# Regrouping the expert rows of a two-layer encoder: sorted lists of 80 and 40 rows, 8 rows whole, gate passes of 80 and 48 rows

## The chip, the cores and the metric

The kernel runs on one core of one Trainium2 chip. The metric is the device time of one execution in microseconds; the profile gives the span from the first to the last instruction, and at each point what the engines did. The engines are named as in the profile: PE is TensorE (with PEld, its weight loads), DVE VectorE, ACT ScalarE, POOL GpSimd and SP SyncE.

## The reference

Two layers, each a token mixer (two attention branches, gates, an output projection) and then PEER, a retrieval feed-forward over 128 x 128 = 16384 experts. The change lies in PEER alone. For 256 tokens, in two chunks of 128:

```python
q = (xc @ w_query).reshape(PEER_CHUNK, PEER_HEADS, 2, half)
s = jnp.einsum('thpk,pnk->thpn', q, sub_keys).astype(jnp.float32)
sv, si = lax.top_k(s, PEER_TOPK)
...
top_s, sel = lax.top_k(cand, PEER_TOPK)
eidx = jnp.take_along_axis(cidx, sel, axis=-1)
g = jax.nn.softmax(top_s, axis=-1)
u = expert_down[eidx]
vv = expert_up[eidx]
act = jax.nn.gelu(jnp.einsum('td,thkd->thk', xc, u).astype(jnp.float32), approximate=False)
return jnp.einsum('thk,thkd->td', (g * act).astype(x.dtype), vv)
```

Each token picks 8 heads x 16 experts. Expert e = 128 i + j; i is called its row here.

## The kernel before, in words

The kernel does not gather per token. In the **downs** (L1313 to L1315) it multiplies all 256 tokens with every row of `expert_down`: 64 blocks of two rows, so 128 units, each of 24 matmuls of 256 columns. GELU (L1253, L1257) is put on the result, in the tile `act` (128 experts of a row on the partitions, rows and tokens along them). The **gates** (g of each expert and token, zero where it was not picked) are made by one-hot matmuls, in two passes over the tokens of 64 rows each. A group of 8 tokens builds a one-hot of j (`ej`, DVE L1026, its scaled copy `el` on ACT L1029), one of i (`ei`, L1031) and two products with g (`ag`, L1035). It then runs 24 matmuls: L1048 (which experts are used, `cnt`), L1051 and L1054 (gates). The result is multiplied into `act` (L1067, L1071, or L1263 where the gate was there before the GELU).

Then the **ups** (L1347) multiply `act` with `expert_up`. A block is 128 experts; each chunk of 128 tokens that uses a block costs one block pass of six matmuls of 512 columns. So that few blocks are needed, rows are sorted. For each list of rows a **rank** is worked out from `cnt` (`rank_lane`: PE L1112, L1117 and L1121, a copy on ACT L1114, DVE L1124 to L1133): used experts get places in the order "first chunk only, both, second chunk only". Then POOL **sends** each row of `act` with one indirect DMA to its places in DRAM (L1161). SP **reads back** sorted blocks (L1191), and POOL **fetches** the 128 rows of `expert_up` that belong to a block with one indirect DMA (L1220). `LISTS` holds for each list: first row, rows, blocks in all, blocks that the first chunk uses, and the block from which the second chunk starts. The rows of `WHOLE` are not sorted: a row is a block as it stands, used by both chunks, and fetched by SP with a plain DMA (L1217).

Each weight or expert block is loaded into `raw` (4 buffers, and 6 more inside `act` during the ups) and **split** into two parts, `wh` (ACT L189) and `wl` (DVE L192); a block of `act` is split the same way (ACT L1236, DVE L1238). Splits run up to four units ahead of PE.

Every engine works through its instructions in the order in which they were written. That order comes from a planner (`Lanes`), which keeps an estimated clock for PE, DVE and ACT and places each step where these clocks say it is ready; `main(emit, 0.655, u)` is the planner's cost of six matmuls. A send is tied to a split by `pace`, so that sends are spread over time. If a list has more used experts than its blocks hold, a slow path (`make_up`) does the rest.

In the ups of each layer list 0 comes first, a block for both chunks and a block for one in turn; then the whole rows, then list 1 in the same turns, and at the end list 1's blocks for the second chunk alone (8 of them, before and now).

Of the kernel before, what the change touches and what calls it, by code (L numbers as in the profile page):

```python
# [10 lines left out]
F32 = mybir.dt.float32  # L11
F32R = mybir.dt.float32r
F16 = mybir.dt.float16
# [42 lines left out]
def vcost(n):  # L56
    return 0.1 + n * 0.00105


def scost(n):  # L60
    return 0.12 + n * 0.00084


class Lanes:
# [8 lines left out]
    def __init__(self):  # L73
        self.clk = {"p": 0.0, "v": 0.0, "s": 0.0}
        self.lanes = []
        self.urgent = 0
# [60 lines left out]
    def idle(self):  # L137
        assert self.lanes
        self.clk["p"] += 0.2
        self.pump()  # L140
# [74 lines left out]
def encoder_kernel(ctx, tc, x_in, wts, downs, ups, gains, gate_bias, qk_norm, rpb, sink, skeys, consts, sums, out,  # L215
# [71 lines left out]
    def main(fn, cost, unit=None):  # L287

        fn()
        lanes.use("p", cost, st.ready[unit] if unit is not None else 0.0)  # L290
        lanes.pump()
# [12 lines left out]
    scr = cpool.tile([128, 704], F32, name="scr")  # L304
# [157 lines left out]
    for l in range(depth):  # L462
# [395 lines left out]
        ejs = [pp.tile([128, 4, 128, 2], F16, name=f"ej{i}") for i in range(2)]  # L858
        els = [pp.tile([128, 4, 128, 2], F16, name=f"el{i}") for i in range(2)]
        eis = [pp.tile([128, 4, 64, 2], F16, name=f"ei{i}") for i in range(2)]  # L860
        ags = [pp.tile([128, 2, 4, 64, 2], F16, name=f"ag{i}") for i in range(2)]
# [94 lines left out]
        def index_lane():  # L956
# [50 lines left out]
            number_experts(64, 128)  # L1007
# [5 lines left out]

        NG = T // 8
        cnts, counted, gates, gelus = {}, [0, 0], [0, 0], [0]

        def gate_group(r, n, o):


            i0, w = LISTS[r][:2]  # L1020
            p0 = 64 * r
            ej, el, ei, ag = ejs[o], els[o], eis[o], ags[o]
            tj = ijT[:, 1, 8 * n:8 * n + 8].rearrange("p (a s) -> p a s", s=2)
            ti = ijT[:, 0, 8 * n:8 * n + 8].rearrange("p (a s) -> p a s", s=2)
            yield ("v", 0.68)
            nc.vector.tensor_tensor(ej, iota2[:, None, :, :].to_broadcast([128, 4, 128, 2]),  # L1026
                                    tj[:, :, None, :].to_broadcast([128, 4, 128, 2]), op=OP.is_equal)
            t1 = yield ("s", 1.04)
            nc.scalar.activation(el, ej, AF.Copy, scale=LOW)  # L1029
            yield ("v", 1.25, t1 - 1.0)  # L1030
            nc.vector.tensor_tensor(ei, iota2[:, None, p0:p0 + 64, :].to_broadcast([128, 4, 64, 2]),  # L1031
                                    ti[:, :, None, :].to_broadcast([128, 4, 64, 2]), op=OP.is_equal)
            for k in range(2):
                tg = gT[:, k, 8 * n:8 * n + 8].rearrange("p (a s) -> p a s", s=2)
                nc.vector.tensor_mul(ag[:, k], ei, tg[:, :, None, :].to_broadcast([128, 4, 64, 2]))  # L1035
# [9 lines left out]
            yield ("p", 0.75)  # L1045
            half, t0 = n // 16, 8 * (n % 16)
            for t in range(8):
                nc.tensor.matmul(cnts[r][:, half * w:(half + 1) * w], ej[:, t // 2, :, t % 2],  # L1048
                                 ei[:, t // 2, i0 - p0:i0 - p0 + w, t % 2], start=counted[r] == 0 and t == 0,
                                 stop=counted[r] == NG - 1 and t == 7, skip_group_check=True)  # L1050
                nc.tensor.matmul(b[:, t * 64:(t + 1) * 64], ej[:, t // 2, :, t % 2],  # L1051
                                 ag[:, 0, t // 2, :, t % 2], start=t == 0, stop=False, skip_group_check=True)
            for t in range(8):
                nc.tensor.matmul(b[:, t * 64:(t + 1) * 64], el[:, t // 2, :, t % 2],  # L1054
                                 ag[:, 1, t // 2, :, t % 2], start=False, stop=t == 7, skip_group_check=True)
# [7 lines left out]
            bv = b.rearrange("p (t i) -> p i t", i=64)  # L1063
            g = min(max(2 * gelus[0] - p0, 0), 64)
            if g < 64:
                t = lanes.use("s", scost(8 * (64 - g)), lanes.cur - 0.5)
                nc.scalar.activation(act[:, p0 + g:p0 + 64, half, t0:t0 + 8], bv[:, g:64], AF.Copy)  # L1067
            if g:
                t = lanes.use("v", vcost(8 * g) - 0.35, t if g < 64 else 0.0)
                a = act[:, p0:p0 + g, half, t0:t0 + 8]  # L1070
                nc.vector.tensor_mul(a, a, bv[:, 0:g])  # L1071
            give(b, "s")
            gates[r] += 1
            if gates[r] == NG:
                for k in range(32 * r, min(gelus[0], 32 * r + 32)):
                    done["row", k] = t

        def gate_lane():
            yield from lane_need(["idx"])
            for r in range(2):  # L1080
                for n in range(NG):
                    o = yield from buf_take("oh")
                    lanes.add(gate_group(r, n, o), after=lanes.cur)

        def rank_lane(r, cnt):
# [5 lines left out]
            def f16(off, n):  # L1091
                return scr.bitcast(F16)[:, 2 * off:2 * off + n]
# [4 lines left out]
            m = f16(256, 4 * w).rearrange("p (k i) -> p k i", k=4)  # L1097
            cs = f16(384, 512).rearrange("p (k j) -> p k j", k=4)
            place = f32(384, 4 * w).rearrange("p (k i) -> p k i", k=4)
            rk = f32(640, w)  # L1100
# [43 lines left out]
        def send_lane(r):  # L1144
# [3 lines left out]

            while r and st.nd < up0 + len([x for x in seq if x[1] == 0]):
                yield None  # L1150
            pace = len(st.splits) - 3.0
            for i in range(i0, i0 + w):
# [17 lines left out]
                pace += (0.4, 0.6)[r]  # L1170
# [73 lines left out]
        def gelu_lane(b, acc):  # L1244
# [4 lines left out]
            r, av = b // 32, acc.rearrange("p (a t) -> p a t", a=2)  # L1249

            g = 8 * gates[r]
# [15 lines left out]
            if gates[r] == NG:  # L1267
                done["row", b] = t
# [32 lines left out]
        for b in range(64):  # L1301
# [4 lines left out]
            for ii in range(2):  # L1306
                h, lo = st.get(u)
                o = acc[:, ii * 256:(ii + 1) * 256]
                for k in range(4):
# [6 lines left out]
                    main(emit, 0.655, u)  # L1316
# [202 lines left out]
```

## Time and profile before

| | |
|---|---|
| median of 3 runs | 1838.83 us (1836.73 to 1839.68) |
| the profiled execution | 1839.15 us, span 1837.3 us |
| clock granted to PE, mean | 0.997 |
| layer 1: downs and ups on PE | 244 to 658, 658 to 925 us of the span |
| layer 2: downs and ups on PE | 1158 to 1572, 1572 to 1834 us |
| block passes in the ups, each layer | 79 (list 0) + 56 (whole) + 45 (list 1) = 180 |

The passes follow from `LISTS`: list 0 has 53 blocks, of which blocks 13 to 38 are used by both chunks (26 x 2) and 27 by one. In a timeline of the profile a row gives start, duration, engine, line, operation, output and input; in brackets stands how long the engine had been idle and what ended that. A PE row's duration overlaps with the next, so the cost of a stream is read from start to start.

### The profile page before, as it was taken

Reading aid. Unit: us, or ns where it says so; the run is one execution under the profiler, and the core shown is the slowest. Engines: PE = TensorE matmul, PEld = TensorE weight load, DVE = VectorE, ACT = ScalarE, POOL = GpSimd, SP = SyncE. Lnnn points to the kernel's source line nnn. Section 1 sums busy time; section 2 is a strip of 40 time slices with the busy share of each in tenths; the row PEclk is TensorE's granted clock in tenths of the full one; section 3 lists DMA queues with packets and bytes.
Section 4 is the critical chain, followed back from the end, with each engine's and each line's share of the span. In section 5 each row is a group of like instructions: output and inputs, shape, how many; then the busy total and the mean of one; then the engine's idle time right before and its main releaser. Section 6 shows DMA issues by size and latency. Waiting matters only on the chain. (4 is left out here: it accounts for less than half of the span.)

```text
span 1837.3 us, 38009 instructions
## 1 busy us (share of the span) xinstructions
PE 1808.9 (98%) x14826; PEld 1646.7 (90%) x14826; DVE 1475.7 (80%) x3054; ACT 1081.3 (59%) x1726; POOL 437.0 (24%) x374
## 2 busy tenths in 40 slices
PE   8999999999999999999999999999999999999998
PEld 7889899999999988888778988999999999888886
DVE  6986899988887897756689778998888888976565
ACT  5665554566566666645546654546666666666554
POOL 0000000000038556744200000000000485567341
PEclk9999999999999999999999999999999999999999
DMA  7535456655567889987464354556554688889873
GB/s 259 166 105 175 149 164 193 187 163 158 155 184 247 242 275 295 323 282 225 161 221 144 108 162 159 165 190 199 159 156 156 189 249 245 277 295 327 260 229 122
DMA packets 125139, 372.98 MB, mean 203 GB/s; under 512 B 16528, under 2 KB 38672, under 8 KB 124944
## 3 DMA queue, kind: packets, MB, share of 16 engines
q1 hardware_dynamic: 91440, 256.93, 45.5%
q0 software_dynamic: 33504, 113.47, 17.9%
q8 instruction: 120, 1.97, 0.4%
q14 instruction: 75, 0.61, 0.1%
HBM read 342.87 MB, written 27.47 MB: 202 GB/s over the span
## 5 line engine op out<-in xcount | busy, mean ns | idle before, releaser
L192 DVE TENSOR_TENSOR wl<-raw,wh 128x1024 fp32r<-128x1024 f32 x478 | 581.0, 1222 | 154.7 <-ACT wh L189 152.8
L189 ACT ACTIVATE wh<-raw 128x1024 fp32r<-128x1024 f32 x478 | 505.8, 1059 | 270.1 <-PE bank L1347 79.0
L1313 PE MATMUL bank<-TT,wh 128*128 128x256 f32 x2048 | 582.9, 285 | 0.0
L1314 PE MATMUL bank<-TT,wh 128*128 128x256 f32 x2048 | 572.2, 279 | 0.0
L1315 PE MATMUL bank<-TT,wl 128*128 128x256 f32 x2048 | 571.5, 279 | 0.0
L1347 PE MATMUL bank<-wh,TT 128*128 128x512 f32 x1416 | 394.7, 398 | 8.6 <-PEq L1362 5.8
L1313 PEld LDWEIGHTS bank<-TT,wh 128*128 128x128 f32 x2048 | 384.8, 188 | 0.3
L1314 PEld LDWEIGHTS bank<-TT,wh 128*128 128x128 f32 x2048 | 384.4, 188 | 0.0
L1315 PEld LDWEIGHTS bank<-TT,wl 128*128 128x128 f32 x2048 | 384.2, 188 | 0.0
L1347 PEld LDWEIGHTS bank<-wh,TT 128*128 128x128 f32 x1416 | 265.0, 188 | 75.3 <-issue 7.2
L1161 POOL DMA_INDIRECT rows<-act,rank x200 | 234.2, 1171 | 371.6 <-DVE miss L1133 311.3
L192 DVE TENSOR_TENSOR wl<-act,wh 128x1024 fp32r<-128x1024 f32 x132 | 161.5, 1225 | 97.2 <-ACT wh L189 90.8
L1347 PE MATMUL bank<-wl,TT 128*128 128x512 f32 x708 | 224.3, 396 | 0.4 <-issue 0.4
L189 ACT ACTIVATE wh<-act 128x1024 fp32r<-128x1024 f32 x132 | 139.7, 1060 | 115.6 <-PE bank L1347 106.8
L871 POOL IOTA act<- 128x128 uint32 x4 | 1.7, 437 | 766.5 <-DVE gT L1005 352.5
L1347 PEld LDWEIGHTS bank<-wl,TT 128*128 128x128 f32 x708 | 133.6, 189 | 32.2
L1029 ACT ACTIVATE el<-ej 128x1024 f16<-128x1024 f16 x128 | 133.8, 1053 | 31.1 <-DVE ej L1026 30.3
L1220 POOL DMA_INDIRECT act<-in_ups_dram,act x96 | 118.0, 1229 | 98.5 <-DVE TT L1238 85.1
L1257 ACT ACTIVATE act<-bank 128x256 f32<-128x256 f32 (+8 forms) x238 | 74.5, 362 | 108.3 <-PE bank L1315 106.4
L435 PE MATMUL bank<-TT,wh 128*128 128x256 f32 x448 | 128.6, 287 | 1.7 <-ACT raw_ka L564 1.0
L437 PE MATMUL bank<-TT,wh 128*128 128x256 f32 x448 | 125.1, 279 | 0.0
L438 PE MATMUL bank<-TT,wl 128*128 128x256 f32 x448 | 125.0, 279 | 0.0
(252 smaller groups left out, 2725.7 us busy)
## 6 DMA issues: line engine op xcount, KB each, us to landing
raw<-in_downs_dram SPq DMA_DIRECT2D x256, 512.0 KB, 4.1
raw<-in_wts_dram SPq DMA_DIRECT2D x132, 512.0 KB, 4.2
act<-in_ups_dram SPq DMA_DIRECT2D x36, 512.0 KB, 5.5
act<-rows SPq DMA_DIRECT2D x82, 129.0 KB, 4.5
raw<-in_ups_dram SPq DMA_DIRECT2D x20, 512.0 KB, 5.5
act<-rows SPq DMA_DIRECT2D x84, 64.5 KB, 5.0
rows<-act,rank POOLq DMA_INDIRECT x200, 5.4
Sq<-in_rpb_dram SPq DMA_DIRECT2D x2, 876.0 KB, 7.1
```

The source lines that it names most:

```text
L189: self.nc.scalar.activation(h, r, AF.Copy)
L192: self.splits.append(self.nc.vector.tensor_sub(lo, r, h.bitcast(F32)).ins.name)
L435: nc.tensor.matmul(o, wh, rh, start=first and i == 0 and pc == 0, stop=False, skip_group_check=True)
L437: nc.tensor.matmul(o, wh, rl, start=False, stop=False, skip_group_check=True)
L438: nc.tensor.matmul(o, wl, rh, start=False, stop=last and i == len(kcs) - 1 and pc == 1, skip_group_check=True)
L1029: nc.scalar.activation(el, ej, AF.Copy, scale=LOW)
L1161: snd = nc.gpsimd.indirect_dma_start(byrank[r], bass.IndirectOffsetOnAxis(ap=rank[:, i:i + 1], axis=0), afl[:, i * ROW:(i + 1) * ROW], None)
L1220: nc.gpsimd.indirect_dma_start(w, None, ups_rows, bass.IndirectOffsetOnAxis(ap=num, axis=0), element_offset=l * 16384 * D)
L1313: nc.tensor.matmul(o, lh, TT[:, :, 0, kc, :], start=kc == 0, stop=False)
L1314: nc.tensor.matmul(o, lh, TT[:, :, 1, kc, :], start=False, stop=False)
L1315: nc.tensor.matmul(o, ll, TT[:, :, 0, kc, :], start=False, stop=kc == 7)
L1347: nc.tensor.matmul(oacc[ch][hf], a, r[:, hf * 512:(hf + 1) * 512], start=first[hf] and a is lh and r is h, stop=last and a is ll)
```

## The change

List 0 grows from 64 rows to 80 (66 blocks, 33 of them for both chunks), list 1 from 36 rows to 40 (33 blocks, 17 for both), and 8 rows instead of 28 stay whole. List 0 has 66 + 33 = 99 block passes, the whole rows 16, list 1 33 + 17 = 50: 165 in each layer. A layer sends 120 rows instead of 100, and splits 107 blocks instead of 111.

The gate passes are cut to fit: pass 0 covers rows 0 to 79 in groups of six tokens (20 of six and 2 of four in each chunk, 44 in all), pass 1 rows 80 to 127 in 32 groups of eight. During pass 0 four sets of one-hot buffers stand ready instead of two; two of them lie in rows of `act` that pass 0 does not use yet (from row 114, `LATE`), and POOL numbers these rows' experts after pass 0.

The sends of list 1 no longer wait until all fetches of list 0 are out. They begin when the first ten blocks are on their way, one for each 1.8 splits. Last, the planner's cost of six matmuls in the downs is 0.7 instead of 0.655.

```diff
-LISTS = [(0, 64, 53, 39, 13), (92, 36, 30, 22, 7)]
-WHOLE = (64, 28)
+LISTS = [(0, 80, 66, 49, 16), (88, 40, 33, 25, 8)]
+WHOLE = (80, 8)
+
+PASSES = [(0, 80, [6] * 20 + [4] * 2), (80, 48, [8] * 16)]
...
+LATE = 114
...
+        oh = [pp.tile([128, 1744], F32, name=f"oh{i}") for i in range(2)] + \
+             [afl[:, i * ROW:i * ROW + 1744] for i in (LATE, LATE + 7)]
...
+            p0, pw, _ = PASSES[r]
...
         def gate_lane():
             yield from lane_need(["idx"])
             for r in range(2):
-                for n in range(NG):
+                if r:
+
+                    while len(free["oh"]) < 4:
+                        yield None
+                    number_experts(LATE, 128)
+                    free["oh"] = deque(x for x in free["oh"] if x[0] < 2)
+                    done["late"] = lanes.clk["p"]
+                else:
+                    free["oh"] = deque((i, 0.0) for i in range(4))
+                for n in range(len(toks[r])):
...
-            while r and st.nd < up0 + len([x for x in seq if x[1] == 0]):
+            whole = up0 + len([x for x in seq if x[1] == 0])
+            while r and st.nd < up0 + DEEP:
                 yield None
...
-                while int(pace) >= len(st.splits) and tries < 15:
+                while int(pace) >= len(st.splits) and tries < 15 and lanes.stuck < 5:
...
-                pace += (0.4, 0.6)[r]
+
+                pace += 0.4 if r == 0 else 1.8 if st.nd < whole else 0.6
...
-                    main(emit, 0.655, u)
+                    main(emit, 0.7, u)
```

How POOL's queue reads in the ups of the first layer. Before, from list 0's sends (L1161, `rows` is the sorted copy in DRAM) through its last fetches (L1220):

```order
L1161 DMA rows_2250<-act,rank 8192x258 x64
L1220 DMA raw<-in_ups_dram,act 128x1024 x4
L1220 DMA act<-in_ups_dram,act 128x1024 x6
```

```order
L1220 DMA raw<-in_ups_dram,act 128x1024 x3
L1161 DMA rows_2251<-act,rank 4608x258 x36
L1220 DMA raw<-in_ups_dram,act 128x1024 x3
L1220 DMA act<-in_ups_dram,act 128x1024 x6
L1220 DMA raw<-in_ups_dram,act 128x1024 x4
```

The same place now (sends are L1183, fetches L1243):

```order
L1183 DMA rows_2244<-act,rank 10240x258 x80
L1243 DMA raw<-in_ups_dram,act 128x1024 x4
L1243 DMA act<-in_ups_dram,act 128x1024 x6
L1243 DMA raw<-in_ups_dram,act 128x1024 x2
L1183 DMA rows_2245<-act,rank 5120x258
L1243 DMA raw<-in_ups_dram,act 128x1024
L1183 DMA rows_2245<-act,rank 5120x258 x2
L1243 DMA raw<-in_ups_dram,act 128x1024
L1243 DMA act<-in_ups_dram,act 128x1024 x2
L1183 DMA rows_2245<-act,rank 5120x258
```

There are now 80 sends ahead of the first fetch instead of 64, and list 1's sends stand between the fetches of list 0 (32 of them there, the last 8 behind its last fetch) instead of in one row of 36 behind them.

How ACT's queue reads where the ups begin in the first layer. `wh<-act` at L1236 is the split of the first sorted block, the `wh<-raw` behind it that of the first block of `expert_up`. Before:

```order
L1029 ACTIVATE el_2244<-ej_2242 128x1024
L1253 ACTIVATE bank_8912<-bank_8912 128x2x200
L1257 ACTIVATE act<-bank_8912 128x2x56
L1236 ACTIVATE wh<-act 128x256
L1236 ACTIVATE wh<-act 128x128
L189 ACTIVATE wh<-raw 128x1024
L1029 ACTIVATE el_2245<-ej_2243 128x1024
```

Now (the split of the sorted block is L1259, that of the unit L194, and L1136 is the copy of list 1's counts in `rank_lane`, L1114 before):

```order
L1043 ACTIVATE oh_2242<-oh_2242 128x1024
L1080 ACTIVATE act<-bank_9304 128x4x8
L1278 ACTIVATE bank_9240<-bank_9240 128x512
L1259 ACTIVATE wh<-act 128x256
L1259 ACTIVATE wh<-act 128x128
L194 ACTIVATE wh<-raw 128x1024
L1136 ACTIVATE scr<-bank_7060 40x512
L194 ACTIVATE wh<-raw 128x1024
```

All gate groups now stand ahead of the first up block, and the copy of list 1's counts stands directly behind that block's split; before, it stood 13 splits later, within the ups. On PE, the matmuls of list 1's rank that wait for this copy stand half a unit ahead of the end of the downs, where before they stood 16 passes into the ups. Counted in PE's order in the same way, the last matmul of list 0's rank stands behind 90 units of the downs before and behind 91.25 now, and the second transposes of the picked indices (L995 before, L1005 now) behind 44.5 units and now 40.75.

More of the change, by code (lines that the diff above doesn't have):

```diff
@@ L75, in __init__ @@
         self.lanes = []
+        self.stuck = 0
         self.urgent = 0
@@ L139, in idle @@
         self.clk["p"] += 0.2
+        self.stuck += 1
         self.pump()
@@ L303, in encoder_kernel @@
     nst = cpool.tile([128, 2, 8], F32, name="nst")
-    scr = cpool.tile([128, 704], F32, name="scr")
+    scr = cpool.tile([128, 832], F32, name="scr")
     def bcast_row(src, off, n):
@@ L857, in encoder_kernel @@
         gT = pp.tile([128, 2, T], F16, name="gT")
[L858 to L861, printed above, removed]
+        oh = [pp.tile([128, 1744], F32, name=f"oh{i}") for i in range(2)] + \
+             [afl[:, i * ROW:i * ROW + 1744] for i in (LATE, LATE + 7)]
+        oh = [x.bitcast(F16) for x in oh]
+        ejs, els = [[x[:, k * 1024:(k + 1) * 1024].rearrange("p (a j s) -> p a j s", a=4, s=2) for x in oh] for k in (0, 1)]
+        eis = [x[:, 2048:2528] for x in oh]
+        ags = [x[:, 2528:3488].rearrange("p (k n) -> p k n", k=2) for x in oh]
         A0 = 64 * ROW
@@ L1010, in index_lane @@
             preload(AF.Gelu)
-        NG = T // 8
+        toks = [[(h, sum(g[:k]), n) for h in range(2) for k, n in enumerate(g)] for _, _, g in PASSES]
         cnts, counted, gates, gelus = {}, [0, 0], [0, 0], [0]
@@ L1044, in gate_group @@
             b, = yield from lane_take("s")
-            yield ("p", 0.75)
-            half, t0 = n // 16, 8 * (n % 16)
-            for t in range(8):
+            yield ("p", 0.095 * nt)
+            for t in range(nt):
                 nc.tensor.matmul(cnts[r][:, half * w:(half + 1) * w], ej[:, t // 2, :, t % 2],
                                  ei[:, t // 2, i0 - p0:i0 - p0 + w, t % 2], start=counted[r] == 0 and t == 0,
-                                 stop=counted[r] == NG - 1 and t == 7, skip_group_check=True)
-                nc.tensor.matmul(b[:, t * 64:(t + 1) * 64], ej[:, t // 2, :, t % 2],
+                                 stop=counted[r] == NG - 1 and t == nt - 1, skip_group_check=True)
+                nc.tensor.matmul(b[:, t * pw:(t + 1) * pw], ej[:, t // 2, :, t % 2],
                                  ag[:, 0, t // 2, :, t % 2], start=t == 0, stop=False, skip_group_check=True)
-            for t in range(8):
-                nc.tensor.matmul(b[:, t * 64:(t + 1) * 64], el[:, t // 2, :, t % 2],
-                                 ag[:, 1, t // 2, :, t % 2], start=False, stop=t == 7, skip_group_check=True)
+            for t in range(nt):
+                nc.tensor.matmul(b[:, t * pw:(t + 1) * pw], el[:, t // 2, :, t % 2],
+                                 ag[:, 1, t // 2, :, t % 2], start=False, stop=t == nt - 1, skip_group_check=True)
             counted[r] += 1
@@ L1062, in gate_group @@
             t = yield ("v", 0.35)
[L1063 to L1067, printed above, removed]
+            bv = b[:, 0:nt * pw].rearrange("p (t i) -> p i t", i=pw)
+            g = min(max(2 * gelus[0] - p0, 0), pw)
+            if g < pw:
+                t = lanes.use("s", scost(nt * (pw - g)), lanes.cur - 0.5)
+                nc.scalar.activation(act[:, p0 + g:p0 + pw, half, t0:t0 + nt], bv[:, g:pw], AF.Copy)
             if g:
-                t = lanes.use("v", vcost(8 * g) - 0.35, t if g < 64 else 0.0)
-                a = act[:, p0:p0 + g, half, t0:t0 + 8]
+                t = lanes.use("v", vcost(nt * g) - 0.35, t if g < pw else 0.0)
+                a = act[:, p0:p0 + g, half, t0:t0 + nt]
                 nc.vector.tensor_mul(a, a, bv[:, 0:g])
@@ L1074, in gate_group @@
             if gates[r] == NG:
-                for k in range(32 * r, min(gelus[0], 32 * r + 32)):
+                for k in range(p0 // 2, min(gelus[0], (p0 + pw) // 2)):
                     done["row", k] = t
@@ L1096, in rank_lane @@
             use = f16(192, 2 * w).rearrange("p (c i) -> p c i", c=2)
[L1097 to L1100, printed above, removed]
+            m = f16(192 + w, 4 * w).rearrange("p (k i) -> p k i", k=4)
+            cs = f16(192 + 3 * w, 512).rearrange("p (k j) -> p k j", k=4)
+            place = f32(192 + 3 * w, 4 * w).rearrange("p (k i) -> p k i", k=4)
+            rk = f32(192 + 7 * w, w)
             if r == 0:
@@ L1248, in gelu_lane @@
             t = yield ("s", scost(512))
-            r, av = b // 32, acc.rearrange("p (a t) -> p a t", a=2)
-            g = 8 * gates[r]
+            if 2 * b >= LATE:
+                yield from lane_need(["late"])
+            r, av = int(2 * b >= PASSES[1][0]), acc.rearrange("p (a t) -> p a t", a=2)
+            g = sum(n for _, _, n in toks[r][:gates[r]])
             if g:
@@ L1266, in gelu_lane @@
             gelus[0] += 1
-            if gates[r] == NG:
+            if g == T:
                 done["row", b] = t
```

33 lines of the change are left out of this document (19 added, 14 removed).

## The prediction

> **What bounds the kernel now.** I read the page's first part first, then the stretches of one layer, then the waits of PE.
>
> ```profile
> PE 1808.9 (98%) x14826; PEld 1646.7 (90%) x14826; DVE 1475.7 (80%) x3054; ACT 1081.3 (59%) x1726; POOL 437.0 (24%) x374
> ```
>
> ```profile
> core 0: us, PE busy (x) PEld busy (x) DVE busy (x) ACT busy (x) POOL busy (x), PEclk, DMA share, GB/s
> 244.00:374.00 130.00, 130.00 (x1107) 130.00 (x1106) 123.84 (x361) 69.79 (x104) 0.00 (x0) 1.00 0.60 187
> 374.00:530.00 156.00, 155.89 (x1888) 154.16 (x1887) 134.96 (x236) 98.29 (x150) 0.44 (x1) 1.00 0.51 157
> 530.00:658.00 128.00, 127.49 (x1555) 126.09 (x1552) 107.35 (x196) 83.32 (x139) 89.72 (x75) 1.00 0.79 241
> 658.00:925.00 267.00, 260.36 (x1213) 207.32 (x1209) 182.36 (x271) 152.98 (x236) 127.76 (x109) 0.99 0.79 256
> ```
>
> ```profile
> PE bank L1347 <- PEq L1362: 5.8, 2, 3.4
> PE bank L355 <- DVE z L393: 3.8, 2, 2.9
> ```
>
> PE is the bound everywhere: it idles 28 of 1837 us, and the longest of its waits adds up to 5.8 us. In the downs (244 to 658) nothing waits at all. DVE is second, at 95% of the first stretch (the top-k), 87% of the second (pass 0 of the gates) and 84% of the third (pass 1). So work taken from PE is gained, as long as no other queue becomes late. The one queue that the change loads in a new way is POOL's, so I read that next, with PE's stream beside it.
>
> ```profile
> 527.65 0.46 PE L1121 MATMUL bank<-scr 64*128 64x64 f16 x10
> 528.05 0.38 PE L1313 MATMUL bank<-TT,wh 128*128 128x256 f32 x1
> ...
> 655.32 0.28 PE L1313 MATMUL bank<-TT,wh 128*128 128x256 f32 x1
> ...
> 655.67 0.28 PE L1313 MATMUL bank<-TT,wh 128*128 128x256 f32 x1
> ...
> 656.49 0.41 PE L1054 MATMUL bank<-ag,el 128*128 128x64 f16 x8
> ...
> 658.25 0.70 PE L1347 MATMUL bank<-wh 128*128 128x512 f32 x2
> 658.79 0.63 PE L1347 MATMUL bank<-wl,wh 128*128 128x512 f32 x2
> 659.26 0.62 PE L1347 MATMUL bank<-wh 128*128 128x512 f32 x2
> ```
>
> List 0's rank ends on PE at 528.05, and the ups begin at 658.25. Three matmuls of the downs take 0.353 us from start to start (655.32 to 655.67), so a unit of 24 takes 2.82. Two of the ups' take 0.47 (658.79 to 659.26), so a block pass of six takes 1.40.
>
> ```profile
> 530.46 2.04 POOL L1161 DMA_INDIRECT rows<-act,rank  x1 [155.66 <-DVE miss L1133]
> ...
> 602.80 1.43 POOL L1161 DMA_INDIRECT rows<-act,rank  x1 [0.30 <-issue]
> ...
> 626.44 0.96 POOL L1161 DMA_INDIRECT rows<-act,rank  x1 [0.30 <-DVE wl L192]
> 637.51 0.97 POOL L1220 DMA_INDIRECT raw<-in_ups_dram,act  x1 [10.11 <-DVE act L1263]
> ...
> 707.07 1.71 POOL L1220 DMA_INDIRECT raw<-in_ups_dram,act  x1 [1.25 <-DVE TT L1238]
> 709.08 0.94 POOL L1220 DMA_INDIRECT raw<-in_ups_dram,act  x1 [0.30 <-issue]
> 711.27 1.71 POOL L1220 DMA_INDIRECT act<-in_ups_dram,act  x1 [1.25 <-DVE TT L1238]
> ...
> 751.08 1.00 POOL L1161 DMA_INDIRECT rows<-act,rank  x1 [0.30 <-issue]
> ...
> 800.10 0.96 POOL L1161 DMA_INDIRECT rows<-act,rank  x1 [0.31 <-issue]
> ```
>
> Behind the rank comes a chain that PE does not see yet. 64 sends run from 530.46 to 626.44, back to back with 0.30 between them: 95.98 us in 63 steps, 1.524 each, and 1.576 over the last 15 steps (602.80 to 626.44). In the ups 36 sends take 35 steps from 751.08 to 800.10, 1.40 each. The first fetch goes out at 637.51, and PE needs its block at 658.25: some 13 us of slack, once landing and split are taken off.
>
> **The change part by part**, for one layer; both layers are alike.
>
> *Block passes.* 180 become 165. 15 x 1.40 = **21.0 us less** on PE, all on the path, since PE is the bound of that stretch. The four splits that go with it lie on DVE and ACT beside PE, worth nothing.
>
> *Gate matmuls.* Pass 0 has the same 768 matmuls (three a token), 80 columns wide for 64. Eight of 64 columns start 0.031 us apart ((0.41 - 0.19) / 7, the last one's own length taken off). By columns, 80 would take 0.039. Nothing at all is the other end, since 0.031 is long for 64 columns beside the downs' 0.118 for 256. I take 5 ns each, +3.8 us, and +1.2 for twelve more groups at 0.1. Pass 1 narrows from 64 to 48, between 0 and -3; I take -1. Together **+4** (0 to +7).
>
> *DVE in top-k and pass 0.* The picked indices are transposed 3.75 units earlier in PE's order, which is 10.6 us; DVE has four splits less before that, 4 x 1.15 = 4.6 us.
>
> ```profile
> 368.75 0.29 DVE L991 TENSOR_TENSOR act<-act 128x128 f32<-128x128 f32 x1
> 368.96 1.22 DVE L192 TENSOR_TENSOR wl<-raw,wh 128x1024 fp32r<-128x1024 f32 x1
> ...
> 371.83 0.49 PE L995 MATMUL bank<-cst,act 128*128 128x128 f32 x3
> ```
>
> DVE was ready at 369.0 and PE came at 371.83; 2.8 - 10.6 + 4.6 makes PE wait 3.2 us. Some of DVE's idle 6 us there may be used up instead, so I take **+2** (0 to +5). In pass 0 DVE gets five more splits (6 us), a quarter more of `ei` and `ag` (10), and 18 more products in the GELU (7): 158 of about 169 us, 93%. That is tight, and still covered by splits that run ahead.
>
> *The handover to the ups.* This is the term that decides. All 80 sends must land before the first read-back. Counted from the end of list 0's rank on PE: first send +2.4 (530.46 - 528.05), 79 steps of 1.524 to the last one, at 122.8.
>
> ```profile
> 633.34 6.64 SPq L1191 DMA_DIRECT2D act<-rows  x12
> DMA to landing us min/median/max: 3.0/5.4/7.2
> DMA to landing us min/median/max: 4.2/5.8/8.5
> 683.70 0.59 ACT L1114 ACTIVATE scr<-bank 36x512 f16<-36x512 f32 x1 [0.47 <-PE bank L1112]
> 686.75 0.30 DVE L1124 TENSOR_TENSOR scr<-bank,scr 128x144 f32<-128x144 f32 x1
> ...
> 688.08 0.27 DVE L1133 TENSOR_REDUCE miss<-scr 128x1 f16<-128x108 f32 x1
> ```
>
> (The landings are those of the sends and of the fetches.) The last send lands 3.0 to 6.9 us later (before, the read-back came 6.9 later, behind a load of the downs in SP's queue); I take 4.0, since the downs' loads are over by then: 126.8. Read-back to fetch +4.2 (633.34 to 637.51): 131.0. The fetch lands 4.2 to 5.8 later, taken as 4.5: 135.5. Then ACT splits the block (1.06), and only then copies list 1's counts (0.59), for which PE waits half a unit ahead of the end of the downs: 137.2. PE's matmuls of that rank (0.6) and DVE's chain for it (686.75 to 688.35, 1.6), which PE waits for once more, and hops bring it to **140**. Without waiting PE would be there at 130: before it took 130.2 (528.05 to 658.25) for 38 units and 28 groups. Now 1.25 units go (-3.5), four groups come (0.83 each, +3.3; -1 as they are narrower), and list 1's rank comes (+1). So PE stands **+10** where it stood for nothing. Ends: at 1.40 a step the stall is gone (-9.8); at 1.576 a step, 6.9 and 5.8 it is 10 + 4.1 + 2.9 + 1.3 = 18. The price of a step is that of the same place in the program, so I keep the middle.
>
> The Trainium skill, in the page "SBUF — State Buffer", section "SBUF: two separate sides", says that GpSimd cannot write the descriptors of its DMAs while DVE holds the port the two share, and waits until DVE is done. The trace agrees: an indirect DMA takes 0.94 to 0.96 us with DVE idle and 1.71 where it starts together with a `wl` split. By that rule a step is 1.26 with DVE idle and no stall follows; with DVE as busy as now, 1.52 stays.
>
> *Sends between fetches.* In list 0's stage a pair of blocks takes PE 4.20 us (707.07 to 711.27), and POOL two fetches, 3.25 with gaps. Now 1.11 sends a pair come in (one per 1.8 splits). At 1.40 each of 3.11 steps is 4.35, at 1.26 it is 3.92, and with a full 1.40 on top of 3.25 it is 4.8. Over the 27 pairs behind the first fetches this is 0 to 16 us too slow; some 8 us of it are covered, as ten blocks are fetched ahead. I take **+1** (0 to +8).
>
> ```profile
> 682.00:751.00 69.00, 69.00 (x308) 54.99 (x307) 50.76 (x78) 42.99 (x66) 42.68 (x33) 1.00 0.88 288
> 751.00:806.00 55.00, 55.00 (x237) 44.32 (x236) 34.84 (x46) 31.17 (x47) 39.32 (x36) 1.00 0.96 327
> ```
>
> DMA carried 288 GB/s there. 32 sends of 132 KB in 139 us add 30: 318, under the 327 that the second row shows without PE waiting.
>
> *The rest.* The iota behind pass 0 (0.4 us on POOL), wider `scr` and two more buffer sets lie beside other work, and the last blocks of a layer stay as they are. Nothing.
>
> Sum: -21 + 4 + 2 + 10 + 1 = -4 a layer, -8 in all. The profiled execution took 1839.15 us (1.85 more than its span), 0.3 above the median of 1838.83, so the forecast is **1831 us**. A measurement of this kernel tells 0.2%, 3.7 us, from no change.
>
> **The rivals.**
>
> *A: the handover costs nothing.* If DVE leaves POOL more room at the end of the downs and a step is 1.40, the stall goes: -21 + 4 + 2 = -15 a layer, 1809 us. For it: the sends of the ups ran at 1.40 with DVE less busy. Against: the rate is the same in both layers, and steps got longer towards the end (1.576), when `act` is multiplied most.
>
> *B: slower, by the handover alone.* The first block's arrival behind 80 sends decides from a stall of 16 us a layer on, that is a mean step over 1.60 with the rest as taken, or 1.576 with the late landings. With a stall of 18 the sum is +4 a layer: 1847 us. For it: the last 15 steps at 1.576, and the added sends are at that end. Against: the downs' loads are over by then.
>
> *C: POOL cannot carry fetches and sends together.* At 4.8 us a pair PE waits in list 0's stage, +8 a layer instead of +1: 1845 us. For it: a fetch that starts with DVE's split took 1.71. Against: a late POOL finds its buffers free, and DVE slows with PE.
>
> *D: the change does not shorten PE's work,* because a list overflows and the slow path runs: hundreds of us. Counted from the reference's inputs, list 0 fills 65.2 and 65.4 of 66 blocks, list 1 32.8 and 32.8 of 33, so it does not.
>
> **How the numbers follow.** The forecast's case 0.55 (1820 to 1840, by half the ends of its terms), A 0.17, B 0.16, C 0.11, D 0.01. Faster by over 0.2% means under 1835.2: 0.75 of the first case and A, 0.58. Within 0.2%: most of the first case's rest, and edges of B and C, 0.17. Slower: 0.25. The range of 1806 to 1850 takes in A, B and C, and leaves out all terms at their best, D, and handover and POOL both at their worst.
>
> **What would show it.** Right: 990 matmuls at the ups' line in each layer; PE idle in one piece of about 10 us at the last half unit of the downs, released by ACT's copy of counts; 80 sends about 1.52 apart; a first fetch some 131 us behind the rank. Wrong: no such gap (A), one of 16 or more (B), or PE waiting for `wh` or `raw` again and again within list 0 (C). A wait at the second transposes shows the top-k term. Were DVE to fall behind in pass 0, the rank itself would come later than PE's work explains, and the forecast would be too low.

## The result and the profile after

| | before | after |
|---|---|---|
| median of the runs beside each other | 1839.26 us (1836.73 to 1840.12, 4 runs) | 1825.78 us (1823.00 to 1827.72, 4 runs) |
| ratio | | 0.9928 (95%: 0.9911 to 0.9945) |
| span of the profiled execution | 1837.3 us | 1821.2 us |
| layer 1: downs, ups (us) | 414.3, 267.1 | 433.5, 238.5 |
| layer 2: downs, ups (us) | 414.4, 260.5 | 433.7, 235.4 |

The change makes the kernel 13.5 us faster; the forecast was 8. The runs came from several chips, and on two of them the kernel before took 1945 to 1950 us instead of 1839; runs from these two, called slower chips below, are set only against runs on the same chip.

The profiled execution of after is the fastest of its four (1823.00 us), so differences read from its rows add up to some 16 us, not 13.5.

The page of after, and then the stretches of layer 1 as before (top-k, pass 0, pass 1 beside the sends, ups; busy time of PE, PEld, DVE, ACT, POOL):

```profile
PE 1774.6 (97%) x14646; PEld 1619.0 (89%) x14646; DVE 1476.7 (81%) x3196; ACT 1084.8 (60%) x1784; POOL 503.6 (28%) x448
```

```profile
244.40:364.30 119.90, 118.74 (x1003) 117.92 (x1002) 117.91 (x355) 63.64 (x93) 0.37 (x1) 1.00 0.57 181
364.30:541.50 177.20, 176.31 (x1997) 174.26 (x1996) 157.64 (x315) 110.33 (x195) 0.19 (x1) 1.00 0.49 155
541.50:677.90 136.40, 127.43 (x1671) 125.70 (x1668) 109.75 (x236) 88.32 (x145) 102.45 (x88) 0.96 0.74 223
677.90:916.40 238.50, 234.03 (x999) 186.40 (x999) 164.41 (x230) 143.93 (x224) 147.31 (x131) 1.00 0.87 298
```

PE's busy time falls by 34 us, and its idle time grows from 28 to 47. DVE (the third engine in each row) has 98% of the top-k stretch and 89% of pass 0. The third stretch holds 9 us in which PE does nothing. The waits of PE (total, times, longest) name it:

```profile
PE bank L1143 <- ACT scr L1136: 18.8, 2, 9.9
...
PE bank L1340 <- DVE wl L197: 2.2, 8, 0.4
...
PE bank L1372 <- ACT TT L1259: 1.6, 2, 0.9
...
PE bank L1372 <- PEq L1387: 1.0, 2, 0.6
```

L1143 is list 1's rank, half a unit ahead of the end of the downs; L1136 is ACT's copy of counts, stuck behind the split of the first block. It is the one big wait. PE's timeline there, and the windows around it (the granted clock is the third number from the end):

```profile
665.52 0.24 PE L1139 MATMUL bank<-scr 128*128 128x160 f16 x1
674.73 0.51 PE L1143 MATMUL bank<-scr 40*128 40x40 f16 x10 [8.97 <-ACT scr L1136]
...
677.26 0.41 PE L1338 MATMUL bank<-TT,wh 128*128 128x256 f32 x1
677.47 0.41 PE L1339 MATMUL bank<-TT,wh 128*128 128x256 f32 x1
...
677.99 0.89 PE L1372 MATMUL bank<-wh 128*128 128x512 f32 x2
```

```profile
675.00:678.00 3.00, 3.00 (x22) 2.86 (x18) 2.60 (x9) 1.06 (x1) 2.09 (x4) 0.50 1.01 385
678.00:679.00 1.00, 1.00 (x6) 0.87 (x6) 0.80 (x2) 0.86 (x2) 1.00 (x1) 0.81 1.08 416
679.00:700.00 21.00, 21.00 (x92) 16.99 (x91) 16.35 (x24) 14.34 (x22) 15.51 (x16) 1.00 1.04 392
```

After the gap PE runs at half its clock for 3.6 us (from 674.73 to the end of the first row, and 0.38 of the second): two matmuls of the downs start 0.21 us apart (677.26, 677.47) instead of 0.118. The twelve matmuls of the downs that are left, the first up and the joins cost some 1.7 us more. In layer 2 the clock stays at 0.50 for 4.8 us behind a gap of 9.9, 1.5 of them within the ups. POOL's chain in the same place (first and last send of 80, first fetch), and what ACT waits for:

```profile
544.20 2.15 POOL L1183 DMA_INDIRECT rows<-act,rank  x1 [9.70 <-DVE miss L1155]
...
662.17 0.96 POOL L1183 DMA_INDIRECT rows<-act,rank  x1 [0.30 <-issue]
667.90 0.98 POOL L1243 DMA_INDIRECT raw<-in_ups_dram,act  x1 [4.76 <-DVE wh L1261]
...
673.14 1.06 ACT L194 ACTIVATE wh<-raw 128x1024 fp32r<-128x1024 f32 x1 [5.58 <-DMA raw<-in_ups_dram,act]
674.10 0.57 ACT L1136 ACTIVATE scr<-bank 40x512 f16<-40x512 f32 x1
```

79 steps take 117.97 us, 1.493 each, in both layers. In list 0's stage POOL runs back to back, 1.41 us a step on average (700 to 815) and here three steps to a pair of blocks in 4.19 us, PE's own pace (4.20); a send, two fetches, a send:

```profile
746.08 1.27 POOL L1183 DMA_INDIRECT rows<-act,rank  x1 [0.30 <-issue]
747.66 1.06 POOL L1243 DMA_INDIRECT raw<-in_ups_dram,act  x1 [0.30 <-issue]
749.02 0.94 POOL L1243 DMA_INDIRECT raw<-in_ups_dram,act  x1 [0.30 <-issue]
750.27 1.28 POOL L1183 DMA_INDIRECT rows<-act,rank  x1 [0.30 <-issue]
```

### The profile page after: what moved, and what is told of

Read it like the earlier page. It is cut to its first block, busy times and chain, and to the rows that moved or that the text cites. A ratio compares the mean times of both kernels' runs of the same rounds, so it can differ in the third digit from the quotient of the medians.

```text
span 1821.2 us, 37929 instructions
## 1 busy us (share of the span) xinstructions
PE 1774.6 (97%) x14646; PEld 1619.0 (89%) x14646; DVE 1476.7 (81%) x3196; ACT 1084.8 (60%) x1784; POOL 503.6 (28%) x448
## 3 DMA queue, kind: packets, MB, share of 16 engines
q8 instruction: 119, 1.95, 0.4%
## 5 line engine op out<-in xcount | busy, mean ns | idle before, releaser
L194 ACT ACTIVATE wh<-raw 128x1024 fp32r<-128x1024 f32 x476 | 503.1, 1058 | 252.7 <-PE bank L1372 60.9
L1372 PE MATMUL bank<-wh,TT 128*128 128x512 f32 x1296 | 358.4, 396 | 5.1 <-DVE TT L1261 2.1
L1183 POOL DMA_INDIRECT rows<-act,rank x240 | 280.6, 1169 | 92.5 <-issue 62.8
L1372 PEld LDWEIGHTS bank<-wh,TT 128*128 128x128 f32 x1296 | 242.3, 188 | 69.5 <-DVE TT L1261 6.1
L197 DVE TENSOR_TENSOR wl<-act,wh 128x1024 fp32r<-128x1024 f32 x126 | 154.4, 1226 | 81.3 <-ACT wh L194 81.2
L1372 PE MATMUL bank<-wl,TT 128*128 128x512 f32 x648 | 204.8, 395 | 0.8 <-issue 0.8
L194 ACT ACTIVATE wh<-act 128x1024 fp32r<-128x1024 f32 x126 | 133.4, 1060 | 103.0 <-PE bank L1372 90.0
L1243 POOL DMA_INDIRECT act<-in_ups_dram,act x118 | 132.3, 1121 | 74.2 <-issue 28.1
L1372 PEld LDWEIGHTS bank<-wl,TT 128*128 128x128 f32 x648 | 121.7, 188 | 29.4
L1282 ACT ACTIVATE act<-bank 128x256 f32<-128x256 f32 (+12 forms) x214 | 65.5, 351 | 80.3 <-PE bank L1340 78.0
L1043 ACT ACTIVATE oh<-oh 128x1024 f16<-128x1024 f16 (+2 forms) x108 | 102.0, 958 | 14.5 <-DVE oh L1040 13.4
```

The costliest lines, as they stand in the source:

```text
L194: self.nc.scalar.activation(h, r, AF.Copy)
L197: self.splits.append(self.nc.vector.tensor_sub(lo, r, h.bitcast(F32)).ins.name)
L1183: snd = nc.gpsimd.indirect_dma_start(byrank[r], bass.IndirectOffsetOnAxis(ap=rank[:, i:i + 1], axis=0), afl[:, i * ROW:(i + 1) * ROW], None)
L1243: nc.gpsimd.indirect_dma_start(w, None, ups_rows, bass.IndirectOffsetOnAxis(ap=num, axis=0), element_offset=l * 16384 * D)
L1372: nc.tensor.matmul(oacc[ch][hf], a, r[:, hf * 512:(hf + 1) * 512], start=first[hf] and a is lh and r is h, stop=last and a is ll)
```

## Experiments: the handover to the ups

Theory H: the gap is the arrival of list 0's first block behind 80 sends, and whatever gives PE other work there gains it back. Its rivals say that the work used as cover is missed elsewhere, or that the wait only moves.

**Whole rows first.** In `blocks_of`, and list 0's end counted accordingly:

```diff
-        seq = []
+        seq = [(l, None, i, (0, 1)) for i in range(WHOLE[0], sum(WHOLE))]
...
-                seq += [(l, None, i, (0, 1)) for i in range(WHOLE[0], sum(WHOLE))]
...
-            whole = up0 + len([x for x in seq if x[1] == 0])
+            whole = up0 + len([x for x in seq if x[1] != 1])
```

> The changed kernel with its 8 whole rows ahead of list 0 in the ups instead of between the lists. Theory H (the gap of 9.0 and 9.9 us at the end of the downs is list 0's first block arriving late behind 80 sends, and the half clock behind it, 1.7 us, is its consequence): the 16 whole passes, 22.4 us, cover it, PE has no gap over 1 us there, and each layer loses 10.8 and 11.6 us: about 1803 us (1800 to 1808). Rival R (the whole rows only lend their cover: where they stood they hid list 1's last sends, read-back and fetch): the wait comes back at the start of list 1, up to 10 us a layer: 1815 to 1826 us.

This run came from a slower chip: 1942.66 us, 0.9956 (0.9940 to 0.9972) of the kernel before there. So it was run again, beside the changed kernel:

> The changed kernel once more, beside the kernels of this call, since the four runs before it came from a chip on which the kernel before took 1950 us and a send 1.88 us instead of 1.52 with PE idle again and again for no reason that the profile names. If that belongs to that chip, this run gives 1823 to 1828 us, a step of 1.49 and a gap of 9 to 10 us a layer, as the first run did. On that same chip the longer step makes 79 sends 31 us longer than here and the gap with it some 25 to 30 us a layer: about 1985 to 2000 us, slower than before there.

> The 8 whole rows ahead of list 0, as in the run before, now with the unedited changed kernel beside it. Theory H (they cover the late first block, 22.4 us a layer): 10.8 and 11.6 us a layer less than the unedited one, about 1803 us, and no gap over 1 us at the end of the downs. Rival R (the wait comes back at the start of list 1): at most half of that gain. On the chip of the run before, where the gap is longer than the cover, about 45 us less than the unedited one.

The changed kernel took 1826.35 us (0.9933, 0.9916 to 0.9949), with a step of 1.493 and the gap of 9.6 and 10.5 us, so it repeats (the half clock behind the first gap lasts 6.5 us there). With the whole rows first it took 1814.84 us (0.9867, 0.9851 to 0.9884): 11.5 less. Both theories are half right: H has the mechanism at the first place, R the size. PE of the kernel with whole rows first at the end of the downs, its largest wait, and POOL around the end of list 1's sends (lines stand one lower than in after):

```profile
667.57 0.28 PE L1339 MATMUL bank<-TT,wl 128*128 128x256 f32 x1
668.70 0.16 PE L1158 MATMUL bank<-miss,scr 128*128 128x2 f16 x1 [0.84 <-DVE miss L1154]
668.72 0.48 PE L1371 MATMUL bank<-wh 128*128 128x512 f32 x1
```

```profile
PE bank L1371 <- ACT TT L1258: 9.6, 2, 5.3
```

```profile
819.33 1.08 POOL L1182 DMA_INDIRECT rows<-act,rank  x1 [0.30 <-issue]
825.54 0.98 POOL L1242 DMA_INDIRECT act<-in_ups_dram,act  x1 [5.13 <-DMA act<-rows]
```

The gap is 0.8 us, and with no half clock behind it: from rank to ups 127.1 us in both layers, instead of 137.1 and 138.0, so 10.0 and 10.9 are gained, as H has it. But the ups take 4.0 and 4.6 us more. Between the lists nothing now covers the last send (819.33), its landing and the first fetch (825.54), and PE waits 4.3 and 5.3 us at the first block of list 1, with half the clock behind it (0.50 from 832.75 to 837.4).

**Whole rows first, list 1's sends earlier.** On top of it:

```diff
-                pace += 0.4 if r == 0 else 1.8 if st.nd < whole else 0.6
+                pace += 0.4 if r == 0 else 0.7 if len(st.splits) < s0 + 8 else 2.0 if st.nd < whole else 0.6
```

> The 8 whole rows ahead of list 0, and list 1's sends begun earlier: one for each 0.7 splits while the whole rows run, then one for each 2.0, so that the last of the 40 goes out ahead of list 0's last fetch instead of four sends behind it. Theory (what came back at the start of list 1, 4.5 and 5.4 us, is the chain last send, landing, read-back, fetch, landing, split, about 14 us, which now begins with ten blocks, 21 us of PE, in hand): that wait goes, the rest stays: 1815 - 10 = 1805 us (1802 to 1809). Rival (POOL has no room for more sends while the first fetches go out, so list 0's blocks come late instead): 1810 to 1818 us with waits in list 0.

1831.88 us (0.9960, 0.9947 to 0.9973): 17 more than without. It is what the rival says, but more of it: its 1810 to 1818 us was too low by 14. The wait at list 1 is gone, but within list 0 PE waits eleven times, and POOL no longer keeps its 1.40:

```profile
PE bank L1372 <- ACT TT L1259: 10.6, 11, 2.8
```

```profile
715.61 1.82 POOL L1243 DMA_INDIRECT raw<-in_ups_dram,act  x1 [0.30 <-issue]
717.74 0.99 POOL L1183 DMA_INDIRECT rows<-act,rank  x1 [0.30 <-issue]
719.03 1.98 POOL L1243 DMA_INDIRECT raw<-in_ups_dram,act  x1 [0.30 <-issue]
```

There are no idle gaps here, only longer instructions: 1.66 us a step over 15 of them (716 to 741), 1.50 over the whole stage (679 to 823). What makes them longer shows beside DVE's rows. In the changed kernel 54 of the 82 transfers from 700 to 815 start within a `wl` split, on average 0.33 us ahead of its end, and take 1.17 us; here 11 of the 17 from 715 to 742 do, 0.72 ahead of its end, and take 1.55. So POOL has fallen out of step with the splits. That the sends put ahead made it late, and that it cannot catch up since it runs without a pause already, is the reading of this; no run tests it by itself.

**Four whole rows first, four between.** `seq = rows_[:4]`, `rows_[4:]` between the lists, and list 0's end counted accordingly.

> Four of the 8 whole rows ahead of list 0 and four between the lists, sends paced as in the changed kernel. Theory (the late first block needs 10 to 12 us of cover, list 1's start 5; each four whole rows are 11.2 us; and POOL's rate in list 0 stays as it was): both gaps go, 1826 - 2 x 10.8 = 1804 us (1801 to 1809), with at most 1 to 2 us of waits in list 0 a layer. Rival (the gap at the end of the downs gave POOL a lead that list 0 needs, as with the planner's cost at 0.72): the gap goes and waits of 4 to 9 us a layer come up late in list 0: 1811 to 1822 us.

A slower chip: 1944.75 us, 1.0002 (0.9975 to 1.0029) of before there. A send took 1.84 us, and the first fetch went out 162 us behind the rank instead of 126, far more than four rows cover. So this stays open.

## Experiments: what sets the rank, the sends and POOL's step

**The planner's cost at 0.72.** One number in `main(emit, 0.7, u)`.

> The planner's cost of six matmuls of the downs at 0.72 instead of 0.70. By PE's order list 0's rank then stands behind 86.25 units of the downs instead of 91.25 (14.1 us of PE earlier) and the first gates behind 41.0 instead of 43.25. Theory (the gap hangs on where the rank stands against the ups, and DVE has room in pass 0): the gap of 9.5 us and the half clock behind it go, and 3 to 4 us a layer come back as PE's wait for DVE in the top-k stage, which is 98% busy: about 1811 us. Rival (DVE cannot make the one-hots of pass 0 that much earlier, and PE waits there instead): 1822 to 1830 us.

1826.09 us (0.9918, 0.9890 to 0.9946; 5 runs, 1817 to 1830): no gain over the changed kernel. The place of the rank did what it should. PE's rows at the rank and at the start of the ups, and its first two waits:

```profile
531.10 0.53 PE L1143 MATMUL bank<-scr 80*128 80x80 f16 x10
...
672.45 0.28 PE L1340 MATMUL bank<-TT,wl 128*128 128x256 f32 x1
672.57 0.62 PE L1372 MATMUL bank<-wh 128*128 128x512 f32 x2
```

```profile
PE bank L1372 <- ACT TT L1259: 9.6, 9, 1.9
PE bank L1340 <- DVE wl L197: 6.0, 10, 1.3
```

The rank comes 10 us earlier (of the 4.1 us missing to 14.1, 3 are PE's waits for `wl` splits in the top-k, as expected), there is no gap ahead of the ups, and the downs are 7.2 us shorter in each layer. The ups give it back: they take 3.7 and 9.3 us more, in waits late in list 0. POOL there:

```profile
746.36 1.73 POOL L1243 DMA_INDIRECT raw<-in_ups_dram,act  x1 [0.30 <-DMA act<-in_ups_dram,act]
748.39 1.81 POOL L1243 DMA_INDIRECT raw<-in_ups_dram,act  x1 [0.30 <-issue]
750.51 1.76 POOL L1183 DMA_INDIRECT rows<-act,rank  x1 [0.30 <-issue]
752.58 1.84 POOL L1243 DMA_INDIRECT raw<-in_ups_dram,act  x1 [0.30 <-DMA act<-rows]
```

Up to 746 a step is 1.40 as in the changed kernel; then it is 1.67 over 15 steps, and the 12 of 16 transfers that start within a split (0.68 ahead of its end) take 1.51. So both the theory and its rival failed: the wait moved, but into list 0, not into pass 0.

**The planner's cost back at 0.655.**

> The changed kernel with the planner's cost of six matmuls of the downs back at 0.655. By the order three gate groups and list 1's rank go behind the first ups again. Theory: the time of the first block's arrival does not hang on it, so PE waits at the first up instead of at list 1's rank, about 12 us for 9.5, and runs three groups (2.5 us) later: 1826 us, within 4. Rival: the gain of 4.8 us that came with list 1's early rank (the wait of 3.4 and 2.4 us for the flag of the slow path, and the half clock behind it in layer 1) goes back with it, and list 1's sends begin 20 us later: 1830 to 1836 us.

> The planner's cost back at 0.655, on a chip with the short step. By the order list 0's rank stands behind 100.25 units of the downs instead of 91.25, 25.4 us of PE later, and only three gate groups (2.5 us) go behind the first ups for it. Theory (the gap is counted from the rank): the rank comes 24 us later, the first fetch too, the ups begin some 21 to 25 us later a layer: 1868 to 1880 us. Rival (the cost only reorders, the rank's place costs nothing): 1826 us, within 5.

Both runs fell on slower chips: 1999.18 us (1.0237, 1.0214 to 1.0261 of before there) and 1993.69 (1.0242, 1.0203 to 1.0281). What both theories of the first expectation left out is the rank's place. Up to the rank these chips show the times of the first ones; the rows are PE's in the second run, and in the kernel with four rows first (cost 0.7) on the same chip:

```profile
565.34 0.53 PE L1143 MATMUL bank<-scr 80*128 80x80 f16 x10
```

```profile
541.35 0.53 PE L1144 MATMUL bank<-scr 80*128 80x80 f16 x10
```

24.0 us later, as the order says. But it is not what the ups wait for here. The first fetch goes out at 713.27, only 9 us later than in the kernel with four rows first (703.96), and the ups begin at 742.21. In between PE has nine gate groups to do, all behind the last matmul of the downs (712.63). The largest of its waits, over both layers, is for DVE's one-hots, and most of it lies there:

```profile
PE bank L1061 <- DVE oh L1045: 37.6, 15, 8.6
```

The last six of these groups come 2.37 us apart, where a group alone costs PE 0.6 (19.8 us for 32). So with the new passes and 0.655 the order leaves gate groups behind the downs, one after the other at the pace of DVE and ACT, and neither theory of either expectation has this. Against the kernels with 0.7 on the same chips (1942.66 and 1944.75) it is 57 and 49 us; but those have whole rows first, which hide part of a late first block, and the changed kernel itself was not run there. So what 0.7 earns in the changed kernel was not measured.

**Sends in one row.** `while r and st.nd < whole:` instead of `up0 + DEEP`, so list 1's sends start behind list 0's fetches.

> The changed kernel with the sends of list 1 in one row behind list 0's last fetch, as the kernel before had them. If sends between fetches are what makes 8 whole rows enough: 40 sends at 1.40 are 56 us, then landing, read-back, fetch, landing and split about 14, together 70 us, and PE has ten fetched blocks (21 us) and 16 whole passes (22.4) to go on with: a wait of 20 to 27 us a layer at list 1, about 1870 to 1880 us. If POOL can be late there for nothing: 1826 us, or about 2 less, since the wait of 1.0 us at the end of list 0 goes as well.

> The changed kernel with list 1's sends in one row behind list 0's last fetch, once more, on a chip with the shorter step if it is one. 40 sends at 1.40 are 56 us, the chain behind them 14 to 17, together 70 to 73 us against 43 us of work that PE has in hand: a wait of 20 to 27 us a layer at list 1, with the half clock behind it, less 1 us of waiting at the end of list 0 that goes: 1865 to 1880 us. Rival (at 1.26 a step, with DVE less busy, and a chain of 12: a wait of 15 to 19): 1855 to 1865 us. If interleaving earned nothing: 1826 us.

On a slower chip 1970.54 us (1.0097, 1.0080 to 1.0113 of before there); on another one 1867.61 us (1.0156, 1.0141 to 1.0170). There the last send stands at 844.45 and PE's wait is in one piece, 21.9 and 21.8 us:

```profile
PE bank L1372 <- ACT TT L1259: 43.7, 2, 21.9
```

As expected: sends between fetches are what makes 8 whole rows enough, worth 41 us (1867.61 - 1826, on two chips that gave the kernel before 1839 and 1840).

**Fewer products on DVE.** In pass 1 the matmuls take `ei` in place of `ag`, and the product into rows with their GELU is left out; first in both layers, then in layer 2 alone:

```diff
-            for k in range(2):
+            for k in range(0 if r and l else 2):
...
-                nc.vector.tensor_mul(a, a, bv[:, 0:g])
+                if not (r and l):
+                    nc.vector.tensor_mul(a, a, bv[:, 0:g])
```

> The changed kernel without the products of pass 1 on DVE: its matmuls take the one-hot of i instead of its product with g, and nothing is multiplied into rows whose GELU is already there (the gates of rows 80 to 127 are left out of the result; counts, lists and sends stay). About 36 us of DVE's 109 in the stretch of list 0's sends go. Theory P (a send costs 1.26 us alone, and more the more DVE works): a step falls from 1.493 to between 1.36 and 1.44, the last send comes 4 to 10 us earlier, and the gap at the end of the downs shrinks by as much: 1806 to 1818 us. Rival (the queue or the landing sets the step): a step stays at 1.49 and the gap at 9 to 10 us: 1826 us, within 4.

> The changed kernel with the products of pass 1 left out on DVE in layer 2 alone (gates of rows 80 to 127 are missing from the last layer's result; counts, lists, sends and layer 1 stay as they are, so layer 1 is the comparison within the run). About 36 us of DVE's 109 in the stretch of list 0's sends go. Theory P (a send costs 1.26 us alone and more the more DVE works): a step is 1.49 in layer 1 and 1.36 to 1.44 in layer 2, whose gap shrinks by 4 to 10 us: 1815 to 1822 us in all. Rival (the queue or the landing sets the step): 1.49 in both, 1825 us.

The first one (on a slower chip, 2641.56 us, 1.3552) tells nothing: with layer 1's gates changed, layer 2 picks other experts, and the slow path runs (443 us of PE's waits). The second took 1824.96 us (0.9922, 0.9905 to 0.9939). The stretch of 80 sends in layer 1 and in layer 2 of that run:

```profile
544.20:662.20 118.00, 118.00 (x1576) 116.87 (x1575) 102.41 (x214) 83.36 (x138) 93.92 (x80) 1.00 0.74 223
1450.50:1565.90 115.40, 115.40 (x1523) 114.21 (x1522) 75.41 (x118) 80.96 (x136) 91.32 (x80) 1.00 0.77 228
```

DVE falls from 87% to 65%, the step only from 1.493 to 1.461; the gap shrinks from 10.5 (in the changed kernel beside it) to 6.7 us. Theory P is wrong in its size: not DVE's busy time counts, but which instructions are in it. POOL and DVE of the changed kernel (its second run), side by side:

```profile
570.63 1.03 POOL L1183 DMA_INDIRECT rows<-act,rank  x1 [0.30 <-issue]
571.96 1.49 POOL L1183 DMA_INDIRECT rows<-act,rank  x1 [0.30 <-issue]
```

```profile
570.25 0.30 DVE L1084 TENSOR_TENSOR act<-act,bank 128x144 f32<-128x144 f32 x1 [1.83 <-ACT act L1080]
...
571.40 1.22 DVE L197 TENSOR_TENSOR wl<-raw,wh 128x1024 fp32r<-128x1024 f32 x1
```

The send at 571.96 starts within a `wl` split and takes 1.49; the one at 570.63 does not. Of the 80 sends of layer 1, the 29 that start within a `wl` split take 1.40 on average (0.97 to 2.15), the 13 others within the one-hot of j (L1040, two SBUF inputs as well) 1.31, the 8 within a product that reads a bank (L1084) 0.96, the 10 with DVE idle 0.96. One that starts within a split takes what is left of the split and some 0.83 more (at 571.96 there are 0.66 left). So the splits make 29 x 0.44 = 12.8 of the 18.4 us that 79 steps take over 1.26 each, and they were all still there; the products that the run leaves out (L1049) are running when 12 of the sends start, and these take 1.17, together 2.5 more than at 0.96: the stretch got 2.6 shorter. The Trainium skill, in the page "SBUF — State Buffer", section "SBUF: two separate sides", has the same distinction: against a GpSimd operation that reads SBUF, a DVE operation with two SBUF inputs takes the port that the two share. This trace agrees, 0.96 us beside an operation that reads a bank, 1.40 beside a split.

## Why the prediction was right, point by point

**Block passes, -21.0.** Right: 990 matmuls at L1372 in each layer. From start to start the line lost 24.7 and 21.2 us; without the waits told below, 21.2 and 20.0.

**Gate matmuls, +4.** Right in sum, not in its parts. 80 columns start 0.038 us apart where 64 did 0.030: pass 0 costs +5.8, against +5.0 with its twelve more groups, whose joins cost nothing that the rows show. Pass 1 saves 3.7 instead of 1. Together +2.1.

**DVE in top-k and pass 0, +2.** The size was right (1.8 and 1.7), the place not: PE waits at four `wl` splits a layer ahead of the second transposes, not at these. DVE did not fall behind in pass 0. The forecast's 158 us of DVE there was right (157.64), but not the 169 us beside it: 156 and five more units (14.1) and +5 for the gates make 175, the stretch took 177.20, and so DVE had 89%, not 93. Ahead of the rank PE waits some 0.7 us more than before, for counts and a table; not forecast.

**The handover, +10.** The mechanism was as told, a single gap released by ACT's copy; with the half clock it cost 10.8 and 11.7. That the size came out so near is luck: two errors met, and a third term was missing. From the rank's end (541.5), forecast and measured in layer 1: last send 122.8, 120.7 (a step of 1.493, not 1.524); first fetch 131.0, 126.4 (5.7 us from the last send, not 8.2); copy of counts done 137.2, 133.2; ups 140, 136.5. The chain was 3.5 us shorter than forecast, and PE's own work was shorter, too: without gap and half clock it would have begun the ups at 125.7, not 130, most of it since the 32 narrower groups of pass 1 cost no more there than 28 did before (19.8 us for 20.4), where the forecast had +2.3. The half clock behind a gap (some 1.7 us a layer) was left out. The Trainium skill, in the page "TensorE: Matmul & The Clock Gate", section "Part 1: The HAM clock gate", states it, half the clock after at least one idle window of about 3.4 us, and at least one busy one of about 3.4 us to get it back. The traces agree on the way back, 0.50 for 3.6 and 4.8 us behind gaps of 9.0 and 9.9, and for 6.5 behind one of 9.6; but the clock fell sooner, at 668.1, 2.4 us into the first gap.

**Sends between fetches, +1.** Right: 0.9 and 0.8 us at the end of list 0, and nothing before. But it hung on more than the forecast saw. POOL had no pause above 0.6 us in that stage (700 to 815), and DVE's splits come at PE's own pace, so that 1.40 is a pace that it can keep or lose; in two experiments it lost it and rival C's price was paid (ups 3.7 and 9.3 us longer at 0.72, 7.0 and 5.1 with list 1's sends earlier). The forecast took DMA for the limit to watch; it carried 392 GB/s with PE fully busy.

**Left out: the flag of the slow path.** At 6.4 us over both layers (5.5 in the second run of the changed kernel, which waits 1.2 and 0.7) it makes up the 5.5 between forecast and result. The flag says whether a list overflowed, and PE's sequencer reads it at a branch at the end of the ups; the first row is before, the second the clock behind it there, the third after:

```profile
902.18 0.93 PE L1347 MATMUL bank<-wh,TT 128*128 128x512 f32 x2 [3.38 <-PEq L1362]
```

```profile
902.00:905.00 3.00, 2.82 (x7) 2.28 (x8) 1.23 (x1) 0.25 (x1) 0.00 (x0) 0.58 0.21 83
```

```profile
894.86 0.70 PE L1372 MATMUL bank<-wh,TT 128*128 128x512 f32 x2 [0.57 <-PEq L1387]
```

2.8 us and 1.6 of half clock are gained in layer 1, 2.0 in layer 2. The row of the waits stood in the prediction (5.8, 2, 3.4), with no term for it. That list 1's rank is earlier now is not the reason: the flag was long done before, too, and with the cost back at 0.655, where that rank stands within the ups again (at 767.35, the ups from 742.21), the wait is 0.6 and 0.5. What goes with it is the loading of instructions. At each of these waits (25 above 0.25 us in all the traces) a 16 KB packet of the instruction queue (q8 on the page) lands 1.5 to 1.8 us before PE starts again. In layer 1 it started 0.9 us after PE ran dry before (899.69 and 898.80), and 2.1 us ahead of that after (892.24 and 894.29). What makes it earlier stays open, and of the kernel before there is one trace only.

In sum for layer 1: -21.2 + 2.1 + 1.8 + 0.7 + 10.8 + 0.9 - 4.4 = -9.3, measured -9.5 (downs and ups together); for layer 2: -20.0 + 2.1 + 1.7 + 0.7 + 11.7 + 0.8 - 2.0 = -5.0, measured -5.8. In the second run of the changed kernel it is -6.9 and -5.6.

**The rivals.** A (handover free) and B (slower by it alone) did not come: the gap was neither gone nor 16. C did not come in this kernel, and came in the two experiments in which POOL lost its pace. D did not come.

## What to carry to other kernels

When a row of DMAs on one queue must end before the first consumer can start, count the whole chain (steps, landing, read-back, fetch, landing, split) from the event that releases it, and put beside it the work that the consumer has in hand; here the sends moved between the fetches earned 41 us, and the order brought the release 24 us forward, at a price that was not measured by itself. Work used to cover one such chain is missed at the next: 22.4 us of whole rows moved ahead gained 10 to 11 us and lost 4 to 5 in each layer. An engine that runs without a pause at exactly the consumer's pace has no reserve, so look at its step, not only at the consumer's waits, before giving it more.

## What the runs showed of the hardware

- PE idle for 9.0 us came back at 0.50 of its clock for 3.6 us, idle for 9.6 us (second run) for 6.5. A wait of 2.44 us in layer 2 of the kernel before left the clock at 1.00, and one of 3.38 in layer 1 did not (0.58). But the length of the wait alone does not decide it: behind one of 1.93 us at 1709.83, in the kernel with the cost at 0.72, the clock was 0.50 from 1711.4 to 1714.7.
- An indirect DMA takes POOL 0.96 us beside a DVE operation that reads a bank, and up to 2.15 when it starts within a split with two SBUF inputs. One that starts within a split takes what is left of it and some 0.83 us more. Three of them to 4.20 us kept in step with DVE's splits at 1.41 a step, starting 0.33 us ahead of a split's end on average; in the two kernels in which this was lost they started some 0.7 ahead, and a step took 1.5 to 1.67.
- On two chips the kernel before took 6% more (1945 and 1950 us for 1839). There, from the first indirect send on and not before it, PE's rows show idle gaps of some 0.5 and 1.2 us with no releaser, and the mean step of a send was 1.75 to 1.95 us; a send with DVE idle took 0.96 as elsewhere, so the time was lost between sends (on average 1.09 of a step of 1.84 in the kernel with four rows first). What causes it stays open.
